# Delta rule and attention encoder on one core: the order of the matmuls taken from an estimate of all engines, outputs of four chunks at once, squares summed in batches, decay tables made inside each batch

## The chip, the core and the metric

The kernel runs on one core of one Trainium2 chip. The core has five engines that run at the same time and meet at semaphores: TensorE (PE in the profile; its weight loads have a row of their own, PEld), VectorE (DVE), ScalarE (ACT), GpSimd (POOL) and SyncE (SP), which here only issues DMAs. ACT issues DMAs too. Each engine works through its own instructions in a fixed order. The metric is the device time of one execution in microseconds, the median of several runs.

## The reference, cut to what matters

One step of a two-layer streaming encoder on 1024 prompt frames and 64 sample frames, all float32. Layer 0 has gated convolutions and chunk-band attention of 8 heads. Layer 1 is a gated DeltaNet with 8 heads of 128 x 128; its frames are cut into chunks of 64, and each chunk needs the state S that the chunk before it left:

```python
def gdn_chunk(S, q, k, v, g, beta):
    gc = jnp.cumsum(g, axis=1)
    ...
    decay = jnp.exp(jnp.where(incl, gct[..., :, None] - gct[..., None, :], -jnp.inf))
    kk = jnp.einsum('blhd,bmhd->bhlm', k, k)
    a = jnp.where(strict, bt[..., :, None] * kk * decay, 0.0)
    tmat = a + jnp.eye(L, dtype=a.dtype)
    rhs = jnp.swapaxes(jnp.concatenate([v * beta[..., None], k * (beta * jnp.exp(gc))[..., None]], axis=-1), 1, 2)
    sol = lax.linalg.triangular_solve(tmat, rhs, left_side=True, lower=True, unit_diagonal=True)
    u = sol[..., :HD_C] - jnp.einsum('bhlk,bhkv->bhlv', sol[..., HD_C:], S)
    qk = jnp.einsum('blhd,bmhd->bhlm', q, k) * decay
    o = jnp.einsum('blhk,bhkv->blhv', q * jnp.exp(gc)[..., None], S) + jnp.einsum('bhlm,bhmv->blhv', qk, u)
    k_dec = k * jnp.exp(g_last[:, None, :] - gc)[..., None]
    S_new = jnp.exp(g_last)[..., None, None] * S + jnp.einsum('blhk,bhlv->bhkv', k_dec, u)
    return S_new, o
```

q and k are L2-normalised before this, and o goes through an RMS norm per head, is multiplied by silu(z) and projected back to 1024 channels. Each layer adds an RMS-normalised result to x.

## The kernel before

**The stages.** Frames lie along the free axis in three groups of 384, 384 and 320 columns. A projection of one weight tile (128 output channels) and one group is 24 matmuls: 8 slices of the contraction, three matmuls each, since weights and activations are split into a high and a low part (`whi`, `wlo`, `hhi`, `hlo`). The core runs, one after the other: the input norm and the projections of layer 0 with the attention of head pairs between them (`even`), the output projection of layer 0 with its norms (`out`), layer 1 (`odd`: convolution tiles of q, k, v per pair of heads with the delta rule between them, then 8 `gate` tiles of z), and the output projection of layer 1. The weights stream in through `stage` on SP's queue; ACT makes the high part and DVE the low part.

**The order of PE.** Only PE's order is written out by hand; the other engines' instructions are ordered by a scheduler of the language. PE's order comes from `Order`: every piece of work is a generator with a rank, and `Order.run` always advances the piece of the lowest rank that is due. A generator yields a number of nanoseconds (not before so long from now), or the name of another piece that must be done first. The piece `main` (rank 5) holds all projections. `project` yields 0 after two of the three matmuls of each slice, and there another piece may step in. The clock of `Order` is a sum of costs that `mm` and `tr` add for PE alone (n / 2.4 + 3 ns for an F32R matmul of n columns); what DVE, ACT, POOL and the DMAs do stands only in the constants that the generators yield, written by hand.

**The delta rule.** A pair of heads p has 17 chunks (16 of the prompt, one of the sample) in batches of 6, 6 and 5, so there are 12 batches. Pieces per batch: `prepare` (rank 2) transposes k and q of each chunk (`tr`), takes the squares' sums with one ACT instruction per chunk (L884), and makes the matrices `An` and `KQD` from `Dst` and `DT`, the decay tables. `substitute` (1.6) inverts 16 x 16 blocks on POOL in 28 small operations (L930, L931), with a DMA to DRAM and back ahead of it (`Sd`, `AL`) and one more pair behind it (`Sd`, `Xf`). `join` (1.5) puts the blocks together in four visits of PE, of which the first needs `XT`, the transpose of what came back. `solve` (1.3) applies the inverse. `scan` (1) goes through the chunks: `ks` = k and q times S, then `us` on DVE (L1079), `su` = the state's update, then the new S on DVE (two operations, L1093). The outputs of a chunk, `up`, are computed ahead of the next chunk's `ks`, added to `qs` on DVE (L1048) and squared on ACT (L1052). `finish` (3) scales four chunks by their norm (one DVE operation per chunk, L1114), transposes them and stores them.

**The decay tables** of all 12 batches are made by the piece `decays` (rank 3) straight after `gates`: per batch one DVE product, one matmul against C_BD, one DVE difference, then two POOL operations (L841), two ACT exponentials and two DMAs to DRAM (`Dd`) on ACT's queue. `prepare` loads its two tables back on SP's queue. The scratch `dbuf` takes one of the two buffers that v uses (`vt`), so `main` waits for `decays` before it makes v of the second pair.

**Waits of main.** q and k of a pair (`kq`) have two buffers, so `main` starts pair p only when `scan` of pair p-2 has ended, and the gates only when the third pair's has.

## Time and profile before

| what | value |
|---|---|
| median of 3 runs | 1499.7 us (1496.54 to 1502.31) |
| the profiled execution, its own time | 1498.51 us |
| its span in the profile | 1496.7 us |
| granted TensorE clock, mean | 0.973 |

The span is the time from the first to the last instruction; 1.8 us of the profiled execution's time lie outside it. Busy time of an engine excludes its DMA issues and its waits. Matmuls overlap, so two matmuls that each take 0.34 us can start 0.17 us apart: where PE is concerned, the distance between starts and the idle time say more than the durations. The granted clock is the share of its full clock that TensorE had; in this profile it is either whole or half.

### The profile page before, as it was taken

Reading aid. Unit: us, or ns where it says so; the run is one execution under the profiler, and the core shown is the slowest. Engines: PE = TensorE matmul, PEld = TensorE weight load, DVE = VectorE, ACT = ScalarE, POOL = GpSimd, SP = SyncE. Lnnn points to the kernel's source line nnn. Section 1 sums busy time; section 2 is a strip of 40 time slices with the busy share of each in tenths; the row PEclk is TensorE's granted clock in tenths of the full one; section 3 lists DMA queues with packets and bytes.
Section 4 is the critical chain, followed back from the end, with each engine's and each line's share of the span. In section 5 each row is a group of like instructions: output and inputs, shape, how many; then the busy total and the mean of one; then the engine's idle time right before and its main releaser. Section 6 shows DMA issues by size and latency. Waiting matters only on the chain. (4 is left out here: it accounts for less than half of the span.)

```text
span 1496.7 us, 28755 instructions
## 1 busy us (share of the span) xinstructions
PE 1376.2 (92%) x10578; PEld 1237.4 (83%) x10578; DVE 858.7 (57%) x2400; ACT 745.6 (50%) x1948; POOL 402.1 (27%) x909
## 2 busy tenths in 40 slices
PE   4899999999999999898876999999989989999995
PEld 3888998999999899887765877778877778888985
DVE  6647237326525755776675667664756665443654
ACT  6544144235325456776655566556555644323642
POOL 4100000000000014432447254452645261410322
PEclk9999999999999999998987999999999999999998
DMA  5231210220211174541332112211211132337454
GB/s 201 83 114 44 77 58 26 87 65 29 74 61 58 44 233 149 180 146 36 94 87 63 31 51 57 42 41 47 67 35 41 37 96 60 99 108 238 154 190 156
DMA packets 114381, 133.15 MB, mean 89 GB/s; under 512 B 35568, under 2 KB 81336, under 8 KB 114240
## 3 DMA queue, kind: packets, MB, share of 16 engines
q1 hardware_dynamic: 82128, 101.86, 22.9%
q10 hardware_dynamic: 32112, 29.45, 6.1%
q8 instruction: 83, 1.36, 0.4%
q14 instruction: 58, 0.48, 0.1%
HBM read 99.91 MB, written 34.51 MB: 90 GB/s over the span
## 5 line engine op out<-in xcount | busy, mean ns | idle before, releaser
L119 PE MATMUL pjt<-hhi,wlo 128*128 128x384 f32 (+1 forms) x1768 | 621.4, 351 | 1.8 <-DVE wlo L162 1.8
L119 PE MATMUL pjt<-hhi,whi 128*128 128x384 f32 (+1 forms) x1768 | 587.5, 332 | 19.7 <-ACT ko L464 4.2
L119 PE MATMUL pjt<-hlo,whi 128*128 128x384 f32 (+1 forms) x1768 | 586.8, 332 | 7.3 <-DVE hlo L215 6.6
L119 PEld LDWEIGHTS pjt<-hhi,whi 128*128 128x128 f32 x1768 | 340.4, 193 | 29.1 <-ACT hhi L214 6.6
L119 PEld LDWEIGHTS pjt<-hhi,wlo 128*128 128x128 f32 x1768 | 340.3, 192 | 26.0 <-issue 12.2
L119 PEld LDWEIGHTS pjt<-hlo,whi 128*128 128x128 f32 x1768 | 339.0, 192 | 10.5 <-DVE hlo L215 8.8
L162 DVE TENSOR_TENSOR wlo<-wf,whi 128x512 fp32r<-128x512 f32 x222 | 155.6, 727 | 138.3 <-ACT whi L161 137.0
L161 ACT CAST whi<-wf 128x512 fp32r<-128x512 f32 x222 | 129.9, 619 | 154.7 <-PE pjt L119 110.9
L544 ACT ACTIVATE pr<-pr,mx 128x640 f32<-128x640 f32 (+5 forms) x72 | 50.9, 706 | 92.7 <-DVE mx L543 92.2
L722 POOL TENSOR_TENSOR kq<-kq,tap 128x384 f32<-128x384 f32 (+1 forms) x64 | 49.7, 784 | 140.5 <-DVE kq L719 99.5
L505 POOL MEMSET bias<- 64x64 f32 x8 | 1.5, 187 | 315.4 <-DMA bias<-Gd 245.0
L345 POOL TENSOR_TENSOR sqa<-sqa,sq 128x384 f32<-128x384 f32 (+1 forms) x36 | 39.7, 1103 | 150.1 <-ACT sq L343 150.0
L541 DVE CUSTOM_DVE_ANT_0 pr<-sc,bias 128x640 f32<-128x640 f32 (+5 forms) x72 | 48.0, 666 | 26.3 <-PE sc L119 22.8
L1093 DVE SCALAR_TENSOR_TENSOR S<-S,egl,su 128x128 f32<-128x128 f32 x128 | 41.1, 343 | 34.9 <-PE su L119 34.3
L930 POOL TENSOR_TENSOR px<-AL 48x14 f32<-48x14 f32 (+6 forms) x168 | 48.6, 289 | 40.0 <-DMA AL<-Sd 31.6
L931 POOL TENSOR_TENSOR AL<-AL,px 48x14 f32<-48x14 f32 (+6 forms) x168 | 52.4, 312 | 8.7
L719 DVE SCALAR_TENSOR_TENSOR kq<-raw,par,kq 128x384 f32<-128x384 f32 (+1 forms) x96 | 48.7, 526 | 9.9 <-ACT raw L715 9.7
L610 POOL TENSOR_TENSOR cvo<-cvo,th 128x384 f32<-128x384 f32 (+1 forms) x12 | 12.0, 999 | 142.6 <-DVE mx L543 113.3
L884 ACT ACTIVATE junk<-tr 128x128 f32<-128x128 f32 x136 | 38.0, 279 | 19.8 <-PE tr L124 16.5
L124 PE MATMUL pt<-cst,pr 128*128 128x128 f32 (+1 forms) x280 | 43.2, 270 | 4.4 <-DVE pr L546 2.9
L119 PE MATMUL pjt<-mhi,whi 128*128 128x384 f32 x128 | 43.5, 340 | 3.1 <-ACT mhi L161 3.1
L119 PE MATMUL pjt<-mlo,whi 128*128 128x384 f32 x128 | 43.7, 342 | 0.3 <-DVE mlo L162 0.3
(240 smaller groups left out, 2344.5 us busy)
## 6 DMA issues: line engine op xcount, KB each, us to landing
wf<-in_w_in SPq DMA_DIRECT2D x128, 256.0 KB, 3.2
wf<-in_w_out SPq DMA_DIRECT2D x96, 256.0 KB, 3.4
mf<-mixd SPq DMA_DIRECT2D x32, 192.0 KB, 3.5
x<-in_x SPq DMA_DIRECT2D x8, 384.0 KB, 5.3
xg<-in_x SPq DMA_DIRECT2D x2, 1536.0 KB
xd<-xg SPq DMA_DIRECT2D x2, 1536.0 KB, 6.9
Dd<-dbuf ACTq DMA_DIRECT2D x16, 192.0 KB, 2.2
od<-o ACTq DMA_DIRECT2D x12, 256.0 KB, 2.5
```

The costliest lines, as they stand in the source:

```text
L119: return self.pe.matmul(out, lhsT=lhsT, rhs=rhs, start=start, stop=stop, **k)
L124: return self.pe.transpose(out, in_, self.ident[0:k, 0:k])
L161: self.act.copy(out=hi, in_=x)
L162: (eng or self.dve).tensor_tensor(lo, x, hi.bitcast(F32), ALU.subtract)
L345: pool.tensor_tensor(acc, acc, sq, ALU.add)
L541: dve.tensor_tensor_reduce(out=cut(pr[0:nq, :nk]), in0=sc[0:nq, :nk // nw, :nw], in1=cut(b["bias"][a][0:nq, j0:j0 + nk]), scale=1.0, scala ...
L544: act.activation(pr[0:nq, :nk], pr[0:nq, :nk], AF.Exp, bias=mx[0:nq, 1:2], scale=1.0, accum_out=mx[0:nq, 2:3])
L719: dve.scalar_tensor_tensor(o, ch(raw[:, i0 + j:i0 + j + m]), cw[j], o, ALU.mult, ALU.add)
L722: pool.tensor_tensor(o, o, ch(t), ALU.add)
L930: pool.tensor_tensor(t, AL[:, j + 1:16, j:j + 1].broadcast_to([lanes, m, w]), x.broadcast_to([lanes, m, w]), ALU.mult)
L931: pool.tensor_tensor(o, o, t, ALU.add)
L1093: dve.scalar_tensor_tensor(Sn[:, q, :], S[:, q, :], egl[:, q, p, c:c + 1], su[q], ALU.mult, ALU.add)
```

## The change

1. **A clock for all engines.** The class `Clock` keeps, for every tensor, when each region was last written and read, and for DVE, ACT, POOL and the DMAs a list of busy spans. `Meter` wraps each engine, so that every operation passes through `Clock.other`, which takes its duration from a fixed part and a part per element; `mm` and `tr` pass through `Clock.tensor`, which waits for its operands and adds 200 ns where the shape of the used array changes. `Pool` wraps the tile pools and tells when a buffer comes free (`turn`).
2. **What generators yield.** No constants any more, but the list of tiles and buffers that the next step needs. `Order.due` takes the latest of their estimated times and adds a margin: 300 ns up to rank 1.1, 1500 ns up to rank 3.5, none for main. `project` now yields twice per slice of the contraction.
3. **Outputs** of up to four chunks become a piece of their own (`out`, rank 2.5): the matmuls of the four, one DVE addition, one ACT square, one DVE sum.
4. **Squares** in `prepare` are taken by one ACT operation per four chunks and summed by one DVE reduction.
5. **Decay tables** are made at the head of `prepare`, in the buffers of `An` and `KQD`, with no DMA; the piece `decays`, its scratch and main's wait for it are gone.
6. `An` is scaled by `sA` on POOL, and `finish` scales its four chunks with one POOL operation. Two DVE operations of `scan` are marked as of high priority for the scheduler. `prepare` of a batch also waits for the outputs of the batch three before it.

The core of the diff:

```diff
+class Clock:
+    FIXED = {"DVE": 170, "ACT": 210, "POOL": 260}
+    EACH = {"DVE": 1.04, "ACT": 0.84, "POOL": 1.9}
+    NEAR, PSUM, DMA, BYTES = 60, 190, 2000, 190.0
...
+    def place(self, eng, t, took):
+        b = self.spans.setdefault(eng, [])
...
+        k = len(b)
+        while k and b[k - 1][1] > t:
+            k -= 1
+        while k < len(b) and b[k][0] < t + took:
+            t = max(t, b[k][1])
+            k += 1
+        b.insert(k, (t, t + took))
+        return t + took
+
+    def tensor(self, out, ins, cost, shape, more):
+        t = max([self.now] + [self.ready(x) for x in ins] + ([] if more else [self.over(out, "PE", False)]))
+        if shape != self.shape:
+            t += 200
+            self.shape = shape
+        self.now = t + cost
...
+    def other(self, eng, op, outs, ins):
+        t = max([self.ready(x, eng) for x in ins] + [self.over(x, eng, False) for x in outs])
+        if "dma" in op:
+            at = self.place("DMA", t, outs[0].nbytes() / self.BYTES if callable(outs[0].nbytes) else outs[0].nbytes / self.BYTES) + self.DMA
+            eng = "DMA"
+        else:
+            n = max(x.free_size() for x in outs[:1] + ins)
+            took = self.FIXED[eng] + self.EACH[eng] * n + (200 if len(outs) > 1 else 0)
+            at = self.place(eng, t, took)
...
 class Order:
+    LATE = ((1.1, 300), (3.5, 1500), (9, 0))
...
+    def due(self, t):
+        at = 0.0
+        late = next(x for r, x in self.LATE if t[0] <= r)
+        for x in t[4]:
+            at = max(at, (x() if callable(x) else self.clock.ready(x)) + late)
+        return at
...
     def project(self, w, ops, n, m=P, ks=range(KT)):
+        yield [self.bank_turn, w[0][:, ks[0], :], ops[0][ks[0]]]
...
             hi, lo = ops[0][k], ops[1][k]
+            yield [w[0][:, k, :], w[1][:, k, :], hi, lo]
             o = ps[0:m, :n]
             self.mm(o, w[0][:, k, :], hi, k == ks[0], False)
             self.mm(o, w[0][:, k, :], lo, False, False)
-            yield 0
+            yield ()
             self.mm(o, w[1][:, k, :], hi, False, k == ks[-1])
...
         def prepare(p, b):
-            nc.sync.dma_start(Dst, Dd[2 * p][:, c0:c0 + nb, :])
-            nc.sync.dma_start(DT, Dd[2 * p + 1][:, c0:c0 + nb, :])
+            An, KQD = bt("An", 64, 2), bt("KQD", 64, 3)
+            Dst, DT = An, KQD
...
+            dve.tensor_tensor(Dst, gcb, cst[:, C_ID64:C_ID64 + 64].unsqueeze(1).broadcast_to(sh), ALU.mult)
+            yield [Dst, turn("tr")]
+            ps = pst("tr")[:, :64 * nb]
+            self.mm(ps, cst[:, C_BD:C_BD + P], Dst.rearrange("p c j -> p (c j)"))
+            dve.tensor_tensor(DT, ps.rearrange("p (c j) -> p c j", j=64), gcb, ALU.subtract)
+            for x, cm, op in ((Dst, C_M1, ALU.subtract), (DT, C_M2, ALU.add)):
+                pool.tensor_tensor(x, cst[:, cm:cm + 64].unsqueeze(1).broadcast_to(sh), DT, op)
+                act.activation(x, x, AF.Exp)
+            yield [kq[:, :, c0:c0 + nb]]
...
-                    for i in range(m):
-                        act.activation(junk, ps[:, i, :], AF.Square, accum_out=ss[:, a, i0 + i:i0 + i + 1])
+                    sq = self.kp.tile([P, 4, P], F32, name="sqk", tag="vr")[:, :m, :]
+                    act.activation(sq, ps[:, :m, :], AF.Square)
...
+                    dve.tensor_reduce(ss[:, a, i0:i0 + m], sq, mybir.AxisListType.X, ALU.add)
...
-                for i in range(m):
-                    dve.scalar_tensor_tensor(An[:, i0 + i, :], ps[:, i, 0:64], sA[:, i0 + i:i0 + i + 1], Dst[:, i0 + i, :], ALU.mult, ALU.mult)
+                ai = An[:, i0:i0 + m, :]
+                dve.tensor_tensor(ai, ps[:, :m, 0:64], Dst[:, i0:i0 + m, :], ALU.mult)
                 dve.tensor_tensor(KQD[:, i0:i0 + m, :], ps[:, :m, 64:128], DT[:, i0:i0 + m, :], ALU.mult)
-                yield 510
+                pool.tensor_tensor(ai, ai, sA[:, i0:i0 + m].unsqueeze(2).broadcast_to([P, m, 64]), ALU.mult)
...
         def scan(p, b):
+                    yield [S, kq[:, :, c], vt[:, c, :], turn("ks")]
                     ks = pst("ks")
...
+                    with tc.high_priority():
+                        dve.tensor_tensor(u, ks[:, 0:P], vt[:, c, :], ALU.add)
+                    act.activation(o4[:, a, :], ks[:, P:2 * P], AF.Copy, scale=egc[:, p, c:c + 1])
-                    yield 850
...
+                yield [u, kd[:, i, :], turn("su")]
...
+        def outputs(p, b, i0, m, o4, u4, us, fresh, f):
+            KQD = R[p, b]["KQD"]
+            yield [*us, o4[:, fresh:m], turn("up")]
+            o = pst("up").rearrange("p (c j) -> p c j", j=P)
+            for i in range(m):
+                for q in range(2):
+                    h = slice(64 * q, 64 * q + 64)
+                    self.mm(o[h, i, :], KQD[h, i0 + i, :], us[i][h], share=1.6, tile_position=(64 * q, 64 * q))
...
+            dve.tensor_tensor(o4[:, fresh:m, :], o[:, fresh:m, :], o4[:, fresh:m, :], ALU.add)
+            act.activation(u4[:, :m, :], o4[:, :m, :], AF.Square)
+            so = self.kp.tile([P, 3, 4], F32, name="so", tag="so", bufs=3)
+            dve.tensor_reduce(so[:, 0, :m], u4[:, :m, :], mybir.AxisListType.X, ALU.add)
+            order.add("fin" + f, 3, finish(p, b, i0, m, o4, so), [])
...
         def finish(p, b, i0, m, o4, so):
-            for i in range(m):
-                dve.tensor_scalar(o4[:, i, :], o4[:, i, :], fa[:, i:i + 1], None, ALU.mult)
-            yield 9000
+            pool.tensor_tensor(o4[:, :m, :], o4[:, :m, :], fa.unsqueeze(2).broadcast_to([P, m, P]), ALU.mult)
+            yield [o4, turn("tr")]
```

Attention and the norms of `out` get lists in place of constants in the same way (before, for instance, the second head's scores waited 1010 ns and the transposes of a unit's probabilities 3000 ns after them).

More of the change, by code (lines that the diff above doesn't have):

```diff
@@ new lines, with __init__, __getattr__, call @@
+class Meter:
+    def __init__(self, clock, eng, real):
+        self._clock, self._eng, self._real = clock, eng, real
+    def __getattr__(self, name):
+        real = getattr(self._real, name)
+        if not callable(real):
+            return real
+        def call(*a, **k):
+            r = real(*a, **k)
+            aps = {i: x for i, x in enumerate(a) if hasattr(x, "tensor")} | {i: x for i, x in k.items() if hasattr(x, "tensor")}
+            outs = [aps.pop(i) for i in ("out", "accum_out") if i in aps]
+            if aps and (not outs or "out" not in k):
+                first = next(iter(aps))
+                outs.insert(0, aps.pop(first))
+            if outs:
+                self._clock.other(self._eng, name, outs, list(aps.values()))
+            return r
+        return call
@@ L90, in run @@
             self.live.sort(key=lambda t: t[:2])
-            free = [t for t in self.live if not (t[5] - self.done)]
-            ready = [t for t in free if t[4] <= self.now]
+            free = [(t, self.due(t)) for t in self.live if not (t[5] - self.done)]
+            ready = [t for t, at in free if at <= self.clock.now]
             if not ready:
-                self.now = min(t[4] for t in free)
+                self.clock.now = min(at for _, at in free)
                 continue
@@ L122, in tr @@
         k = in_.partition_size()
-        self.order.now += 108 if k > 64 else 56
+        self.clock.tensor(out, [in_], 109 if k > 64 else 62, (-(-k // 32), 4), False)
         return self.pe.transpose(out, in_, self.ident[0:k, 0:k])
@@ L218, in open @@
         es = ExitStack()
[L219 removed]
+        p = Pool(self.clock, es.enter_context(self.tc.tile_pool(name=name, bufs=1, **(dict(side=side, reuse_waits="tile") if not k else k))))
         self.opened[name] = es
```

274 lines of the change are left out of this document (153 added, 121 removed).

## The prediction

> **What bounds the kernel now.** I read the page's head first, then busy time by stage, then PE's waits inside the two stages of layer 1 that the change rewrites, then single stretches of the timeline. The stage rows give length and PE, PEld, DVE, ACT and POOL busy (with counts), the granted clock, DMA share and GB/s.
>
> ```profile
> span 1496.7 us, 28755 instructions
> ```
> ```profile
> 100.00:600.00 500.00, 492.63 (x3371) 467.60 (x3369) 257.24 (x687) 211.05 (x486) 31.68 (x38) 1.00 0.24 76
> 600.00:712.00 112.00, 101.70 (x625) 90.52 (x624) 83.37 (x158) 77.43 (x153) 38.05 (x32) 0.96 0.37 121
> 712.00:825.00 113.00, 85.32 (x600) 75.79 (x600) 75.25 (x182) 63.88 (x173) 61.04 (x106) 0.88 0.32 81
> 825.00:1350.00 525.00, 499.07 (x4918) 418.57 (x4918) 310.58 (x1151) 274.14 (x893) 217.97 (x679) 0.98 0.22 59
> ```
>
> PE is the engine to save: in the scan stage (825 to 1350) it is busy 95%, DVE only 59%. The work that PE does hardly changes in amount, so the change can win only PE's idle time, and the half clock that follows it. Attention (100 to 600) leaves 7.4 us idle in 500: little to win there. The ramp into the delta rule (712 to 825) leaves 113 - 85.32 = 27.7 us, the scan stage 525 - 499.07 = 25.9 us; together 53.6.
>
> The half clock: these rows are the stretches at half clock between 702 and 822 us (the first of five, and their sum), then the sum of the three after 1060.
>
> ```profile
> 702.00:712.60 10.60, 8.48 (x86) 8.11 (x86) 5.11 (x16) 4.36 (x9) 1.98 (x2) 0.52 0.01 2
> ...
> sum 38.10, PE 27.91 PEld 24.58 DVE 20.94 ACT 16.29 POOL 18.45; mean PE 5.58 PEld 4.92 DVE 4.19 ACT 3.26 POOL 3.69
> ```
> ```profile
> sum 17.20, PE 12.81 PEld 12.31 DVE 10.53 ACT 8.43 POOL 13.60; mean PE 4.27 PEld 4.10 DVE 3.51 ACT 2.81 POOL 4.53
> ```
>
> Work at half clock takes twice as long, so half of its busy time is lost: (27.91 - 8.48) / 2 = 9.7 us in the ramp (its first stretch is before the delta rule and stays), 12.81 / 2 = 6.4 us later; together 16.1. So 53.6 + 16.1 = **69.7 us is the most** that these two stages can return without PE doing less.
>
> What PE waited for, longest in total, in the ramp and then in the scan stage (us, times, longest):
>
> ```profile
> PE tr L119 <- DVE XT L960: 9.3, 1, 9.3
> PE tr L124 <- DVE dbuf L838: 5.4, 2, 3.7
> PE tr L119 <- DVE kd L887: 4.9, 1, 4.9
> ```
> ```profile
> PE tr L124 <- DVE o L1114: 7.2, 3, 5.3
> ...
> PE tr L119 <- DVE XT L960: 2.9, 2, 1.9
> ...
> PE su L119 <- DVE us L1079: 1.3, 2, 0.9
> ```
>
> These are visits whose written delay was shorter than reality: PE is in order, so a transpose of `finish` sent 5.3 us too early (`o`) stops projections that were ready. The scan itself is almost never late (`us` twice, 1.3 us): its constants are generous.
>
> **The change, part by part.**
>
> *Order from an estimate.* Waits of the kind "my constant did not know that DVE or POOL was busy" should go. What the estimate can't see is an engine's queue held by a DMA: it puts each operation into the engine's next free time. The trace shows such a case, on POOL:
>
> ```profile
> 782.47 0.21 POOL L930 TENSOR_TENSOR px<-AL 48x14 f32<-48x14 f32 x1 [5.14 <-DMA AL<-Sd]
> ```
>
> POOL stood 5.1 us for `AL`; the convolution's additions queued behind it, then DVE, and PE's 4.9 us wait for `kd` followed. The `XT` waits hang on the same chain. The estimate takes 2000 ns plus bytes / 190, for these 48 KB 2.26 us; measured landings (`AL`, then `Xf`):
>
> ```profile
> DMA to landing us min/median/max: 1.6/2.4/5.6
> ```
> ```profile
> DMA to landing us min/median/max: 2.2/3.2/4.8
> ```
>
> The median errs by 0.1 and 0.9 us, inside the margin of 1.5; the slow hops don't. So I keep the waits of this family, 9.3 + 4.9 + 2.9 = 17.1 of 53.6, **32%**, and let the rest go: -36.5 us. The half clock goes in the same share: -10.9. Bounds: nothing kept (-69.7), two thirds kept (-23). What is late next is `AL` and `Xf`.
>
> *Visits.* What it costs PE to leave a projection:
>
> ```profile
> 909.78 0.31 PE L119 MATMUL pjt<-hhi,whi 128*128 128x320 f32 x1
> 909.93 0.31 PE L119 MATMUL pjt<-hlo,whi 128*128 128x320 f32 x1
> 910.17 0.44 PE L119 MATMUL up<-us,KQD 64*64 64x128 f32 x4
> 910.53 0.66 PE L119 MATMUL ks<-S,kq 128*64 128x128 f32 x8
> 911.12 0.42 PE L119 MATMUL pjt<-hhi,wlo 128*128 128x320 f32 x1
> 911.37 0.31 PE L119 MATMUL pjt<-hhi,whi 128*128 128x320 f32 x1
> ```
>
> Projections start 0.15 us apart; the last before the visit has 0.24, the first after it 0.25: about 0.2 us a visit. `up` takes 0.36 for four records, `ks` 0.59 for eight, so four more records cost 0.23. Outputs now: 68 x 0.36 = 24.5 us. After: 68 x 0.23 + 24 visits x (0.13 + 0.2) = 23.5. **Batching the outputs is worth 1 us of PE.** Against it, steps that shared a visit because their constants fell together now come due one by one, and a unit of attention gets a separate visit for its fifth key tile. I take +6 us, some 30 visits; the trace can't show how many, so the bounds are -4 (20 merge) and +15 (75 more). Net +5.
>
> *Decay tables.* Per batch the same two DVE operations, matmul, two POOL operations and two exponentials; 24 stores on ACT's queue and 24 loads on SP's go.
>
> ```profile
> L841 POOL TENSOR_TENSOR dbuf<-cst,dbuf x24: 857/1110/1315, 723.8 to 805.2; 128x384 f32<-128x384 f32 x16, 128x320 f32<-128x320 f32 x8
> ```
>
> All 24 stood in the ramp; now about six do, so some 18 x 1.11 = 20 of POOL's 61 busy us leave it. That is part of why the ramp's waits go and isn't counted again. Main's wait for `decays` is free: with the ramp's waits gone main has eight tiles ahead of it, by the code, and the scan of the first pair runs meanwhile; if that scan ends later than main's tiles, PE idles as long as it is late, inside the range up to some 10 us. The new wait of `prepare` for outputs three batches back costs nothing: a whole batch's scan lies between.
>
> *Squares and scalings.*
>
> ```profile
> L884 ACT ACTIVATE junk<-tr 128x128 f32<-128x128 f32 x136 | 38.0, 279 | 19.8 <-PE tr L124 16.5 <-DVE raw L710 0.6 <-ACT junk L884 0.4
> ```
> ```profile
> L887 DVE TENSOR_TENSOR kd<-tr,dec 128x512 f32<-128x512 f32 x12 | 8.2, 686 | 3.9 <-ACT kt L886 3.8
> ```
> ```profile
> L722 POOL TENSOR_TENSOR kq<-kq,tap 128x384 f32<-128x384 f32 x32 | 32.5, 1015 | 95.9 <-DVE kq L719 61.3 <-DVE so L1108 14.8 <-DVE so L1109 9.0
> L896 POOL TENSOR_TENSOR kt<-kt,kap 128x768 f32<-128x768 f32 x8 | 12.2, 1523 | 5.9 <-DVE sA L894 3.4 <-DVE kap L895 2.4
> ```
>
> ACT loses 136 squares of 279 ns with their read-outs and gets 48 wider ones: relief. DVE gets 48 reductions and 24 for the outputs. No row shows a reduction; the nearest DVE operation of 512 elements takes 686 ns, half of them are that wide, the rest half or less: about 37 us (bounds 20 and 50), which the operations given to POOL and the merged additions about repay. POOL gets 48 scalings, between the rows for 384 and 768 elements 1.2 us at 512: about 37 us. In the scan stage DVE is busy 310.58 and POOL 217.97 of 525, so all lies beside PE: 0, and the rival below if that cover fails.
>
> *Norms of `out`.* Three waits of 600 to 712 hang on the squares' sums and should go: -2 of these 2.8 us.
>
> ```profile
> PE pjt L119 <- POOL sqa L345: 1.0, 1, 1.0
> PE pjt L119 <- ACT sq L343: 0.9, 1, 0.9
> PE pjt L119 <- POOL sqb L314: 0.9, 1, 0.9
> ```
>
> **Sum:** 1496.7 - 36.5 - 10.9 + 5 - 2 = 1452.3 us of span; with the 1.8 us outside it (1498.5 for the profiled execution) **1454 us**. That execution lies 1.2 us below the median of 1499.7, which I neglect.
>
> **The rivals.**
>
> *A. More goes.* The late landings were a result of the crowded ramp and leave with it; 55 to 70 us gone: 1426 to 1440. For it: the typical landings fit the estimate. Against: by the code these DMAs share SP's queue with the weights all along.
>
> *B. POOL holds up DVE.* One DVE operation of 0.31 us median took 1.05 while a POOL addition ran:
>
> ```profile
> 767.87 1.07 POOL L722 TENSOR_TENSOR vt<-vt,tap 128x384 f32<-128x384 f32 x1 [1.02 <-ACT junk L884]
> ```
> ```profile
> 768.00 1.05 DVE L912 SCALAR_TENSOR_TENSOR Af<-An,cst,Af 128x96 f32<-128x96 f32 x1
> ```
> ```profile
> L912 DVE SCALAR_TENSOR_TENSOR Af<-An,cst,Af x36: 284/310/1070, 768.0 to 1268.1; 128x96 f32<-128x96 f32 x24, 128x80 f32<-128x80 f32 x12
> ```
>
> The estimate gives each operation a fixed time. If each of the 48 new POOL scalings (0.77 us on average) holds a DVE operation ahead of a scan step for its whole length, less the 0.3 us margin, that is 48 x 0.47 = 23 us: 1477. Against it: the median of the 36 says that most go free.
> The Trainium skill ("SBUF — State Buffer", Who interferes with whom) says that DVE and GpSimd share one pair of SBUF ports, held by one for a whole instruction, and that a DVE operation with two SBUF inputs contends with GpSimd's reads; it speaks against giving POOL work. The row agrees: 1.05 against 0.31 us.
>
> *C. It doesn't do what it says.* PE's order is planned, but the other engines' order still comes from a scheduler that the estimate doesn't know; the waits move and stay as large: 1498, between 1490 and 1507. Against: the estimate's parts fit the rows closely.
>
> *D. Slower: the scan's margin is too thin.* Before, the scan's steps left 850 and 1110 ns on a clock that ran slow (it gave 136 ns to a matmul that takes 0.15 us). Now a scan step is sent 300 ns after its estimate. DVE is in order and often within a weight split:
>
> ```profile
> L162 DVE TENSOR_TENSOR wlo<-wf,whi 128x512 fp32r<-128x512 f32 x222 | 155.6, 727 | 138.3 <-ACT whi L161 137.0 <-PE tr L124 0.5
> L1079 DVE TENSOR_TENSOR us<-ks,vt 128x128 f32<-128x128 f32 x64 | 18.4, 288 | 20.3 <-PE ks L119 13.8 <-ACT raw L715 6.2
> L1093 DVE SCALAR_TENSOR_TENSOR S<-S,egl,su 128x128 f32<-128x128 f32 x128 | 41.1, 343 | 34.9 <-PE su L119 34.3 <-issue 0.2
> ```
>
> There are 136 scan visits (`ks` and `su` of 68 chunks), and while PE waits nothing else runs. It decides against the change from a mean lateness of 46 / 136 = 0.34 us beyond the margin. A whole split each time, 0.7 us: 95 us, net +49: 1547. For it: DVE is busy 59% of that stage. Against: the estimate allows 190 + 303 + 60 + 300 = 853 ns after `ks` where `us` takes 288, and 1156 after `su` where two S take 686, so half a microsecond is left; and the operations got priority.
>
> **How the numbers follow.** Forecast (1440 to 1475) 0.58; A 0.12; B (1475 to 1492) 0.10; C 0.08; D 0.12. Predicted is the forecast's 1454. Faster by over 0.5% (under 1492; 7.5 us is about what a measurement of this kernel can tell from no change): 0.58 + 0.12 + 0.10 = 0.80; within 0.5% 0.08; slower 0.12. The range: below, A's bound, 1425 (0.03 left out beyond it); above, into C, 1500, with D and the rest of C left out, 0.15.
>
> **What would show each step.** Idle PE between 712 and 1350 falls from 53.6 to some 17 us, with `XT` or what hangs on `AL` first among the waits, and `o` and `dbuf` gone; half clock after 712 is under 15 us; `up` comes in records of 16 and PE's busy time in the scan stage hardly falls per chunk; ACT falls by some 65 us and POOL rises by some 40. It would be wrong if `su` or `ks` head the waits (D), if L1079 or L1093 start late behind POOL (B), if idle time stays near 50 us under other names (C), or if main stands still for a scan to end.

## The result and the profile after

The changed kernel takes 1549.0 us (1541.9 to 1551.3), beside 1501.0 us of the kernel before in the same session: 1.0306 times the time, with a 95% interval of 1.0251 to 1.0361. It is slower by some 48 us, and the forecast of 1454 was wrong in its sign.

The page's head, first; then, from both kernels, busy time by stage, cut at the same events in each: the first matmul of `gates`, the first `su`, the last `su`, the first matmul of the last output projection. Columns as before: window, its length, busy us of PE, PEld, DVE, ACT and POOL with counts, granted clock, DMA share, GB/s.

```profile
span 1549.5 us, 28339 instructions
...
PE 1397.2 (90%) x10578; PEld 1267.6 (82%) x10578; DVE 877.2 (57%) x2320; ACT 732.1 (47%) x1630; POOL 431.4 (28%) x957
```
Before:
```profile
705.00:834.00 129.00, 101.32 (x745) 91.72 (x745) 83.14 (x203) 72.54 (x193) 64.62 (x112) 0.86 0.30 75
834.00:1336.00 502.00, 476.07 (x4766) 396.38 (x4764) 299.97 (x1116) 264.06 (x867) 210.25 (x650) 0.98 0.22 58
1336.00:1369.00 33.00, 33.00 (x205) 32.23 (x204) 11.94 (x33) 9.36 (x22) 5.14 (x24) 1.00 0.50 163
```
After:
```profile
719.00:837.00 118.00, 105.40 (x811) 98.91 (x811) 74.13 (x198) 62.66 (x147) 50.45 (x101) 0.93 0.19 40
837.00:1372.00 535.00, 473.32 (x4615) 398.22 (x4613) 321.75 (x1033) 257.73 (x589) 255.45 (x705) 0.91 0.18 44
1372.00:1417.00 45.00, 45.00 (x278) 44.40 (x278) 14.85 (x38) 11.98 (x26) 6.24 (x26) 1.00 0.46 143
```

The 53 us of span stand in five places. Up to `gates` 14 are lost (705 to 719). The ramp is 11 us shorter (129 to 118), as hoped: its idle PE fell from 27.7 to 12.6 us. The scan stage is 33 longer (502 to 535), and its idle PE is 535 - 473.3 = 61.7 us, before 25.9. Behind it stand 12 more (33 to 45), projections that PE did not get to earlier. The last projection takes the other 5. In the scan stage PE did 151 matmuls less, and the clock fell from 0.98 to 0.91.

Over the whole span, counted in the two traces: PE's idle time went from 120.4 to 152.2 us. Half of the time that PE was busy at half clock is lost; this went from 28.0 to 64.3 us. The rest of PE's busy time, its work at full clock, went from 1348.2 to 1333.0 us. So PE had 15 us less to do and lost 68 us more, over half of that to the clock.

What PE waited for in the scan stage after, longest in total (us, times, longest):

```profile
PE tr L285 <- POOL o L186: 24.5, 8, 4.9
PE su L280 <- DVE u L186: 9.8, 10, 3.0
PE tr L280 <- DVE XT L186: 6.2, 3, 3.7
PE ks L280 <- DMA S<-in_s: 6.0, 4, 2.0
...
PE ks L280 <- DVE S L186: 2.4, 4, 0.9
```

In these waits an instruction had been put into PE's fixed order too early. All waits of this view add up to 60.8 of the 61.7 idle us. They don't show whether PE had anything else to do: there are stretches in which `main` has no projection to offer. PE's timeline at the longest (start, us, tiles; rows left out between):

```profile
912.77 0.31 PE L280 MATMUL pjt<-hhi,wlo 128*128 128x320 f32 x1
913.20 0.53 PE L280 MATMUL tr<-M,X 32*32 32x16 f32 x40
918.09 0.69 PE L285 MATMUL tr<-cst,o 128*128 128x128 f32 x2 [4.36 <-POOL o L186]
...
922.17 2.05 PE L280 MATMUL tr<-BD,kt 128*128 128x128 f32 x8 [0.25 <-DVE BD L186]
...
927.24 0.66 PE L280 MATMUL ks<-S,kq 128*64 128x128 f32 x8
...
946.77 1.06 PE L280 MATMUL tr<-vr,BD 128*128 128x128 f32 x8
947.75 0.44 PE L280 MATMUL up<-u,KQD 64*64 64x128 f32 x4
948.12 0.44 PE L280 MATMUL pjt<-hhi,whi 128*128 128x384 f32 x1
```

For 35 us there is no projection (`pjt`): by the code, `main` has finished the second pair's tiles and waits for the first pair's scan to end before it starts the third's. A second such stand, 32 us, comes before the `gate` tiles. PE has only the delta rule's small steps then, each behind another engine, and much of it runs at half clock: `tr<-BD,kt` takes 2.05 us where its eight matmuls take 1.13 elsewhere. The rows of the two stands:

```profile
913.10:948.10 35.00, 26.56 (x363) 20.55 (x363) 19.09 (x55) 15.71 (x39) 8.00 (x22) 0.71 0.15 35
1227.10:1259.60 32.50, 25.49 (x278) 18.71 (x278) 14.81 (x43) 13.63 (x33) 8.97 (x20) 0.63 0.19 56
```

PE is idle 8.4 and 7.0 us in them, 15.5 of the stage's 61.7. The other 46.2 us lie where projections were at hand; before, the whole stage had 25.9. So the stands are about a quarter of the idle time, and neither kind of loss is the whole.

The scan itself was late. `ks` is its first visit for a chunk; these are its visits on both sides of the border between the first pair's second and third batch, before and after:

```profile
882.93 0.66 PE L119 MATMUL ks<-S,kq 128*64 128x128 f32 x8
905.70 0.61 PE L119 MATMUL ks<-S,kq 128*64 128x128 f32 x8
```
```profile
897.28 0.92 PE L280 MATMUL ks<-S,kq 128*64 128x128 f32 x8
927.24 0.66 PE L280 MATMUL ks<-S,kq 128*64 128x128 f32 x8
```

The scan stands 22.8 us before and 30.0 after, until the third batch is ready. Over the 64 visits of each trace, the 11 distances across a border between batches or pairs add up to 243.9 us before and 260.3 after, and the 52 distances within a batch to 253.7 and 271.5. So batches come later, and within a batch the chunks follow each other more slowly as well, by about the same total. The length of `prepare`, from a batch's first transpose of k to its last `Af`, is read from such rows (batch 2, before, then after):

```profile
834.73 0.66 PE L124 MATMUL tr<-cst,kq 128*128 128x128 f32 x4
...
858.07 0.30 DVE L912 SCALAR_TENSOR_TENSOR Af<-An,cst,Af 128x80 f32<-128x80 f32 x1
```
```profile
842.11 0.66 PE L285 MATMUL tr<-cst,kq 128*128 128x128 f32 x4
...
877.41 0.28 DVE L186 SCALAR_TENSOR_TENSOR Af<-An,cst,Af 128x80 f32<-128x80 f32 x1
```

From 23 to 35 us in this batch; on average over the 12, up to the store of `Af`, from 24.7 to 30.9 us. The decay tables are not in this stretch: they come ahead of the first transpose.

### The profile page after: what moved, and what is told of

It is laid out like the page before. It is cut to its first block, busy times and chain, and to the rows that moved or that the text cites. A ratio compares the mean times of both kernels' runs of the same rounds, so it can differ in the third digit from the quotient of the medians.

```text
span 1549.5 us, 28339 instructions
## 1 busy us (share of the span) xinstructions
PE 1397.2 (90%) x10578; PEld 1267.6 (82%) x10578; DVE 877.2 (57%) x2320; ACT 732.1 (47%) x1630; POOL 431.4 (28%) x957
## 5 line engine op out<-in xcount | busy, mean ns | idle before, releaser
L280 PE MATMUL pjt<-hhi,whi 128*128 128x384 f32 (+1 forms) x1768 | 604.3, 342 | 31.4 <-ACT raw L186 11.7
L280 PE MATMUL pjt<-hhi,wlo 128*128 128x384 f32 (+1 forms) x1768 | 607.9, 344 | 3.1 <-DVE wlo L186 2.9
L280 PEld LDWEIGHTS pjt<-hlo,whi 128*128 128x128 f32 x1768 | 343.1, 194 | 11.1 <-DVE hlo L186 8.8
L186 DVE TENSOR_TENSOR wlo<-wf,whi 128x512 fp32r<-128x512 f32 x222 | 159.7, 744 | 153.6 <-ACT whi L186 152.9
L186 POOL TENSOR_TENSOR sqa<-sqa,sq 128x384 f32<-128x384 f32 (+1 forms) x43 | 44.7, 1040 | 201.7 <-ACT sq L186 184.5
L186 POOL TENSOR_TENSOR so<-so 128x4 f32<-128x4 f32 (+2 forms) x216 | 50.3, 235 | 127.0 <-DVE so L186 116.3
L186 POOL TENSOR_TENSOR px<-AL 48x14 f32<-48x14 f32 (+6 forms) x168 | 53.1, 316 | 41.9 <-DMA AL<-Sd 26.0
L280 PE MATMUL ks<-S,kq 128*64 128x128 f32 x512 | 48.9, 307 | 8.7 <-DMA S<-in_s 6.0
L186 ACT ACTIVATE o<-ks,egc 128x128 f32<-128x128 f32 x64 | 23.5, 367 | 57.9 <-DVE u L186 55.6
L280 PEld LDWEIGHTS ks<-S,kq 128*64 128x64 f32 x512 | 31.7, 148 | 23.1 <-issue 15.4
L186 ACT ACT_TABLE_LOAD x38 | 48.8, 1283 | 3.8 <-DMA Gd<-Ld 2.4
```

The source lines that it names most:

```text
L186: r = real(*a, **k)
L280: return self.pe.matmul(out, lhsT=lhsT, rhs=rhs, start=start, stop=stop, **k)
```

## The experiments

Two theories stood at the start. **PE's waits**: the estimate sends steps too early (to `finish` behind POOL, to the scan behind DVE), and what PE stands idle is lost. **Late batches**: the chain of a batch got longer, `main` runs out of projections and PE has nothing to do. Each run has beside it the kernel before on the same chip; "stage" is the stretch from the first to the last `su`, by the rows of busy time by stage.

| run | us | ratio to before | stage us, idle PE, clock |
|---|---|---|---|
| before | 1501 | 1 | 502, 25.9, 0.98 |
| after | 1549 | 1.0306 [1.0251, 1.0361] | 535, 61.7, 0.91 |
| b_out4 | 1503 | 1.0030 [1.0014, 1.0046] | 502, 32.2, 0.98 |
| b_pool | 1517 | 1.0124 [1.0100, 1.0149] | 519, 37.7, 0.97 |
| b_decays | 1527 | 1.0197 [1.0172, 1.0223] | 550, 46.8, 0.95 |
| order_only | 1540 | 1.0253 [1.0230, 1.0276] | 514, 55.8, 0.92 |
| b_late6 | 1538 | 1.0247 [1.0210, 1.0284] | 538, 45.7, 0.95 |
| b_exps | 1505 | 1.0000 [0.9979, 1.0022] | 506, 28.2, 0.98 |
| b_tables | 1500 | 1.0018 [1.0000, 1.0036] | 503, 26.7, 0.98 |
| o_dve | 1540 | 1.0243 [1.0209, 1.0277] | 516, 60.6, 0.93 |
| late300 | 1550 | 1.0314 [1.0279, 1.0350] | 554, 67.3, 0.91 |
| decays_ahead | 1553 | 1.0341 [1.0313, 1.0369] | 519, 70.2, 0.91 |
| fin9000 | 1552 | 1.0337 [1.0290, 1.0384] | 536, 69.2, 0.91 |
| fin9000_rest300 | 1554 | 1.0344 [1.0292, 1.0396] | 567, 75.2, 0.90 |
| fin9000_scan800 | 1520 | 1.0117 [1.0079, 1.0155] | 531, 50.6, 0.94 |
| fin9000_scan1500 | 1586 | 1.0585 [1.0553, 1.0616] | 604, 99.5, 0.90 |
| scan800 | 1530 | 1.0203 [1.0180, 1.0226] | 527, 50.6, 0.94 |
| odd_fixed | 1619 | 1.0772 [1.0729, 1.0814] | 617, 111.1, 0.89 |
| est_dve | 1554 | 1.0372 [1.0345, 1.0399] | 557, 69.6, 0.90 |
| est_best | 1593 | 1.0637 [1.0605, 1.0669] | 606, 92.4, 0.88 |

### One part of the change alone, on the kernel before

**b_out4.** Outputs of four chunks in one visit, with the priority of the scan's operations, and with delays as before.

```diff
-                if last:
-                    outputs(*last)
+                if a == 3 or i == nb - 1:
+                    order.add("out" + f, 2.5, outputs(p, b, i - a, a + 1, o4, u4, us, ...), [])
```


> The kernel before with one part of the change: outputs of four chunks per visit, with their squares summed in a batch, and priority for the scan's operations; order and delays as before. What the prediction costed at 1 us less of PE: 1495 to 1506. If the new body is harmful by itself: over 1512.

1503 us, slower by 0.3%. PE is busy 469.8 us in the stage instead of 476.1, and idle 32.2 instead of 25.9: what the batching saves of PE, its waits take back.

**b_pool.** The two scalings on POOL.

```diff
-            for i in range(m):
-                dve.tensor_scalar(o4[:, i, :], o4[:, i, :], fa[:, i:i + 1], None, ALU.mult)
+            pool.tensor_tensor(o4[:, :m, :], o4[:, :m, :], fa.unsqueeze(2).broadcast_to([P, m, P]), ALU.mult)
...
+                pool.tensor_tensor(ai, ai, sA[:, i0:i0 + m].unsqueeze(2).broadcast_to([P, m, 64]), ALU.mult)
```


> The kernel before with one part of the change: the scalings of the outputs (per four chunks) and of An done by POOL. The prediction had them beside PE: within 8 us of 1502. If POOL in order is the mechanism (the scalings queue behind a substitution, and what comes behind them waits): `tr` for `o` or for `XT` takes 30 us or more, and the time is 1515 to 1560.

1517 us, slower by 1.24%, inside the range expected for POOL's order as the mechanism, though neither wait reached the 30 us named there. The two largest among PE's waits, over the whole span:

```profile
PE tr L119 <- DVE XT L961: 25.3, 4, 16.1
PE tr L124 <- POOL o L1114: 12.9, 3, 7.9
```

`XT` was 12.2 us before and `o` (on DVE) 7.2. Both hang on POOL, one on the substitution, one on the new scaling: POOL goes through its queue in order, and its load, 234 of 519 us, says nothing of how long the queue is when a batch needs it.

**b_decays.** The decay tables inside `prepare`, with the delays of the old piece.

```diff
-            nc.sync.dma_start(Dst, Dd[2 * p][:, c0:c0 + nb, :])
-            nc.sync.dma_start(DT, Dd[2 * p + 1][:, c0:c0 + nb, :])
+            dve.tensor_tensor(Dst, gcb, cst[:, C_ID64:C_ID64 + 64].unsqueeze(1).broadcast_to(sh), ALU.mult)
+            yield 900
+            ps = pst("tr")[:, :64 * nb]
...
+            yield 2500
```


> The kernel before with one part of the change: the decay tables computed in each batch's prepare. The ramp up to the first `su` gets 5 to 15 us shorter, since 18 of POOL's 24 operations leave it. If the longer chain in each batch and the table loads cost nothing: 1485 to 1500. If they cost what the ramp gives or more: 1500 to 1530, with `XT` or `KQD` first among the waits.

1527 us. Its ramp and its scan stage:

```profile
703.00:810.00 107.00, 92.94 (x732) 86.89 (x732) 63.12 (x185) 58.57 (x170) 43.15 (x91) 0.89 0.17 35
810.00:1360.00 550.00, 503.19 (x4805) 413.88 (x4804) 312.48 (x1140) 303.47 (x913) 229.59 (x670) 0.95 0.18 48
```

The ramp is 22 us shorter and the scan stage 48 longer. What the ramp returns, every batch pays later. The waits are headed by `o` (16.6 us), not by `XT` or `KQD` as expected. `main` never runs out for more than 8 us in this scan stage: its 46.8 idle us, 21 more than before, are mostly PE's waits while projections were at hand, and the clock fell from 0.98 to 0.95. Why, b_late6 and b_exps ask.

**order_only.** The order by the estimate, around the bodies of before (also the decays ahead). The edit is shown against the changed kernel.

```diff
-                    sq = self.kp.tile([P, 4, P], F32, name="sqk", tag="vr")[:, :m, :]
-                    act.activation(sq, ps[:, :m, :], AF.Square)
+                    for i in range(m):
+                        act.activation(junk, ps[:, i, :], AF.Square, accum_out=ss[:, a, i0 + i:i0 + i + 1])
...
+                if last:
+                    outputs(*last)
...
-            pool.tensor_tensor(o4[:, :m, :], o4[:, :m, :], fa.unsqueeze(2).broadcast_to([P, m, P]), ALU.mult)
+            for i in range(m):
+                dve.tensor_scalar(o4[:, i, :], o4[:, i, :], fa[:, i:i + 1], None, ALU.mult)
...
+                        order.add("decays", 3, decays(), ["gates"])
```

> The order from the estimate, with the margins of the changed kernel, around the bodies of before: outputs per chunk inside the scan, squares with their sums on ACT, decays ahead, scalings on DVE and not on POOL. If the bodies are to blame (POOL's scaling, decays, batches of outputs): 1445 to 1475, what the prediction gave for the order alone. If the order itself is (1500 ns at every step of a batch, 300 ns at the scan's): over 1520, with main standing still for a scan to end.

1540 us: the order alone loses 2.5%. But its longest stand is not of the kind expected. `main` stands from 853 to 933 us, and comes back right behind the last matmul of `decays` (932.5). The last of the 24 POOL operations of `decays` starts at 936.8:

```profile
L186 POOL TENSOR_TENSOR dbuf<-cst,dbuf x24: 852/993/1453, 739.1 to 936.8; 128x384 f32<-128x384 f32 x16, 128x320 f32<-128x320 f32 x8
```

In the kernel before the last starts at 805.2. By the code, `decays` has rank 3, and each of its visits waits until one of the two `tr` banks has been free for 1500 ns; every other piece of the batch wants the same banks at a better rank. So this run holds a loss of its own that the changed kernel hasn't, and its 38 us are no clean price of the order.

### Is it lateness, or work?

**b_late6.** The kernel before; each `prepare` starts 6 us later on the order's clock, and nothing else is added.

```diff
-            yield 4000 if b == 0 else 0
+            yield 10000 if b == 0 else 6000
```


> The kernel before, with one number changed: prepare of each batch starts 6000 ns later on the order's clock; no engine does more. If the delta rule goes by when its batches are ready: the scan's stands between batches (258.6 us in all now) grow by 20 to 60 us, main stands for a scan, and the time is 1515 to 1550. If there is slack in the batches, and PE's waits for late operands are what costs: within 6 us of 1500.

1538 us, 2.5% slower, 37 us: no instruction was added, and PE, DVE and POOL have the kernel before's work (counts in the stage of 4761, 1116 and 652 beside 4766, 1116 and 650).

```profile
832.00:1370.00 538.00, 492.26 (x4761) 406.97 (x4759) 297.90 (x1116) 262.81 (x864) 210.54 (x652) 0.95 0.21 55
```

Idle PE went from 25.9 to 45.7 us and the clock from 0.98 to 0.95: both follow from late batches here. The distances between `ks` across a border grew from 243.9 to 273.5 us, within a batch from 253.7 to 260.3. So this run decides one thing: the batches have no slack that 6 us wouldn't use up. It doesn't decide between the theories, since `main` stands only once for more than 8 us:

```profile
926.60:947.40 20.80, 11.85 (x169) 8.04 (x168) 12.28 (x52) 10.12 (x45) 6.51 (x21) 0.61 0.26 49
```
```profile
PE tr L124 <- DVE o L1114: 16.5, 7, 4.5
```

That stand holds 8.9 of the 45.7 idle us. The rest are waits of PE, `o` first, which took 7.2 before: late batches cost through such waits as well.

**b_exps**, and **b_tables** before it. Two exponentials of one column in each batch, to bring in the activation table loads of the decays alone.

```diff
+            for q in range(2):
+                e = self.kp.tile([P, 1], F32, name="e1", tag="e1", bufs=2)
+                act.activation(e, rr[:, q, 0:1], AF.Exp, scale=-1.0)
```


> The kernel before, with two exponentials of one column in each batch's prepare, whose results nothing uses: they add what the decays inside the batch add in activation table loads (from 20 to about 40, 1.28 us each) and nothing else. If the table loads are the cost of the decays: 1515 to 1530. If the longer chain is: within 6 us of 1501.

> The kernel before, with two exponentials of one column in each batch's prepare, tied to the batch by reading its norms; nothing uses their results. Table loads go from 20 to 32 or more. If the loads (1.28 us each on ACT) are the cost of the decays inside the batch: 1512 to 1530. If the longer chain is: within 6 us of 1500.

In b_tables the exponentials read `gc`, which is there from the start; the loads stayed at 20, so they must have been put beside other exponentials, and the run says nothing. In b_exps they read the batch's norms. ACT's groups of table loads, in b_exps and then the same lines of before:

```profile
L729 ACT ACT_TABLE_LOAD x12 | 15.4, 1283 | 0.9 <-ACT dbuf L842 0.8
L895 ACT ACT_TABLE_LOAD x10 | 12.8, 1283 | 0.2
```
```profile
L729 ACT ACT_TABLE_LOAD x3 | 3.8, 1283 | 0.8 <-ACT dbuf L842 0.8
```

That and one more make 40 loads instead of 20, as many as in b_decays. ACT is busy 30 us more (775.6 beside 745.6), and the time is the same, 1.0000 [0.9979, 1.0022]. The Trainium skill ("ScalarE: Activation LUTs", What ACT_TABLE_LOAD costs) gives 1283 ns a load, as the rows do, and 2.66 us for a switch with its drain; by that figure 20 switches would be 53 us, an estimate, if ACT were on the path. The time shows that it isn't: 20 more loads on ACT cost nothing when nothing waits for the exponentials. In b_decays the batch does wait for them, and no run took that alone. What is left for the decays' 30 us, by elimination and so not shown, is the longer way of each batch (two delays of 0.9 and 2.5 us and the work between them, on POOL too) and the waits of PE that follow.

### The margins

Here only `LATE` and, for the scan, its rank change.

```diff
-    LATE = ((1.1, 300), (3.5, 1500), (9, 0))
+    LATE = ((3.5, 300), (9, 0))                                    late300
+    LATE = ((1, 300), (1.1, 800), (3.5, 1500), (9, 0))             scan800, scan at rank 1.05
+    LATE = ((1.1, 300), (2.9, 1500), (3.5, 9000), (9, 0))          fin9000
+    LATE = ((2.9, 300), (3.5, 9000), (9, 0))                       fin9000_rest300
+    LATE = ((1, 300), (1.1, 800), (2.9, 300), (3.5, 9000), (9, 0)) fin9000_scan800; 1500 for 800: fin9000_scan1500
```


> The changed kernel with 300 ns instead of 1500 ns of margin for the batch's steps (solve, join, substitute, prepare, outputs, finish). Late batches by margin: prepare has eight or so visits, each 1.2 us earlier, so a batch is ready some 10 us sooner, the two stands of main (35.6 and 34.1 us) shrink to 20 to 25 each, and the time falls to between 1520 and 1535. Late scaling and thin margin: the transposes of `finish` come sooner after POOL was asked and wait longer, `tr` for `o` goes from 24.5 to over 30 us, and the time is 1549 or up to 15 us more.

> The changed kernel, but `finish` sends its transposes 9000 ns after the estimate has the scaled outputs ready instead of 1500; POOL still scales. Too early a finish: the 24.5 us of waits of `tr` for `o` go, and with each of the eight waits one stretch of about 3.4 us at half clock (1.7 us lost): 1549 falls by 24 to 38 us, to between 1511 and 1525. POOL's load itself: the waits move to what else hangs on POOL (AL, kq, vt) and the time stays above 1540. If only main's two stands for a scan decide, the waits were inside them and the time falls by less than 10 us.

late300: 1550, as without it. Its waits and those of fin9000:

```profile
PE tr L285 <- POOL o L186: 39.6, 11, 7.8
```
```profile
PE tr L280 <- DVE XT L186: 32.3, 7, 13.4
PE su L280 <- DVE u L186: 12.9, 11, 3.0
```

Less margin brings `prepare` down only from 30.9 to 28.8 us and PE into waits for POOL. Main's two stands mostly go: in the scan stage, stretches of over 8 us without a projection add up to 30 us instead of 68, with the same time. A late `finish` takes the `o` waits away (3.4 us are left); PE waits for `XT` instead and `main` stands longer (112 us in all), at 1552. So neither the stands nor one of the waits is what the time hangs on: taking one away moves the loss to the other.

> As fin9000, and with 300 ns instead of 1500 for all the batch's other steps. If the batches' margins and the early finish both cost: main's stands go as they did with 300 ns alone, and no `o` waits come in their place: 1475 to 1500. If the 1500 ns cost nothing (as 300 ns alone, which gave 1550, may say): the same as fin9000 within 8 us.

> The changed kernel with one number changed: the scan's own steps come 800 ns after the estimate instead of 300, all other margins as they were. If the scan's thin margin is the mechanism (PE stands for `u` or `S`, and half clock follows): waits of `su` and `ks` on DVE fall from 12 to under 5 us, half clock between the first and the last `su` by some 10 us, and the time by 15 to 30 us, to between 1519 and 1534. If its gain with the other margins was chance or needs the late finish: 1541 or more.

> As fin9000_rest300, and the scan's own steps 800 ns instead of 300 after the estimate. Thin margin of the scan (the prediction's case of slower): the 12 us of waits of `su` and `ks` go and what follows them at half clock, 10 to 18 us less than fin9000_rest300. If the margin is right: a chunk's two visits come 0.5 us later each, 68 chunks are 68 us longer in a chain that main's projections must fill, main stands longer for a scan, and it is 5 to 20 us more than fin9000_rest300.

> fin9000_scan800 with 1500 instead of 800 ns behind the estimate for the scan's steps. If steps sent too early are what costs: another 5 to 20 us less, 1500 to 1515. If 800 covers them: the scan's chain gets 136 x 0.7 us longer, main runs out of projections and stands longer, 1525 to 1550.

fin9000_rest300: 1554, as fin9000. scan800: 1530, within what the thin margin was expected to cost, but not for its reason. `su` waits for `u` as long as it did:

```profile
PE su L280 <- DVE u L186: 10.0, 13, 2.0
```

Idle PE in the stage falls by 11 us: outside main's two stands from 46 to 27 us, while the stands remain (46 and 25 us). The clock goes from 0.91 to 0.94. `prepare` is as long as without the 800 ns (30.7 us on average), so 19 of the 48 us came back without the batches getting shorter. With the late `finish` and 300 ns elsewhere the same 800 brings 34 us. And 1500 instead of 800 costs 66, more than was expected either way:

```profile
817.00:1421.00 604.00, 504.49 (x4831) 431.95 (x4832) 327.48 (x1060) 266.52 (x614) 246.35 (x712) 0.90 0.17 45
```

99.5 us idle. The chain of 68 chunks is then the later one: the distances between `ks` within a batch add up to 519 us, those across borders to 77.5 (351 and 175 with 800). So there is an optimum that depends on the other margins; where it lies, and why 800 helps, stays open.

### Parts of the change taken back

**o_dve**: the outputs' scaling on DVE again. **decays_ahead**: the piece `decays` again. **odd_fixed**: the new bodies with the old written delays in the delta rule.

```diff
o_dve
-            pool.tensor_tensor(o4[:, :m, :], o4[:, :m, :], fa.unsqueeze(2).broadcast_to([P, m, P]), ALU.mult)
+            for i in range(m):
+                dve.tensor_scalar(o4[:, i, :], o4[:, i, :], fa[:, i:i + 1], None, ALU.mult)
decays_ahead
+                        order.add("decays", 3, decays(), ["gates"])
...
+            nc.sync.dma_start(Dst, Dd[2 * p][:, c0:c0 + nb, :])
+            nc.sync.dma_start(DT, Dd[2 * p + 1][:, c0:c0 + nb, :])
odd_fixed
-                    yield [S, kq[:, :, c], vt[:, c, :], turn("ks")]
...
-                yield [u, kd[:, i, :], turn("su")]
+                if S is not None:
+                    yield 850
...
-            yield [o4, turn("tr")]
+            yield 9000
```

> The changed kernel, with the scaling of the outputs (o4) by DVE per chunk again instead of by POOL per four chunks. Three theories for the 49 us that the change lost. Late scaling: PE's transposes of `finish` wait for POOL, which is in order and busy with a substitution's 28 operations; then the 24.5 us of waits of `tr` for `o` go, with the half clock behind them, and the time falls from 1549 to between 1510 and 1525. Late batches: main runs out of projections because the batches come late for other reasons; then PE waits for something else or stands longer at the ends of main's tiles, and the time stays above 1538. Thin margin of the scan: DVE gets 68 more operations of about 0.2 us ahead of the scan's steps; the waits of `su` and `ks` grow from 12 to some 20 us and the time is 1549 or more.

> The changed kernel with the decay tables computed ahead for all pairs, stored to DRAM and loaded per batch, as before the change. If the decays inside the batch are to blame (activation table loads went from 20 to 38, 1.28 us each, and every batch has a longer chain ahead of its transposes): prepare of the third batch of a pair falls from some 40 to some 28 us, the two stands of main shrink from 35 to 15 us, table loads fall to about 20, and the time is 1510 to 1525. If they are not: within 8 us of 1549, the ramp up to 10 us longer again.

> The changed kernel's bodies, but in the delta rule (gates, prepare, substitute, join, solve, scan, outputs, finish) each step comes a written delay after the last, with the numbers of before (9000 ns for finish, 850 and 1110 for the scan, 2160 per group of prepare); attention and norms keep the estimate. If the estimate in the delta rule is the cause: idle PE plus half clock between the first and the last `su` fall from 101 us to between 35 and 50, and the time to between 1480 and 1500. If the new bodies are the cause (POOL's scalings, decays inside the batch): above 1525.

o_dve: 1540, 9 us less with intervals that overlap, not the 24 and more that its waits had promised; `tr` now waits 14.1 us for `o` from DVE. decays_ahead: 1553, no gain, since the piece starves as in order_only (the last of its POOL operations starts at 905 us). odd_fixed: 1619, on the side expected if the new bodies are the cause (above 1525), but not a clean test of it. The old delays don't fit the new bodies: `XT` alone takes 70.9 us of waits there and `o` 37.1. The estimate is better than those constants for these bodies; it is the old bodies under the old constants that beat both.

**est_dve** and **est_best** start from fin9000_scan800, put both scalings on DVE, and then make the decays ahead (rank 2.9).

```diff
est_dve
-                pool.tensor_tensor(ai, ai, sA[:, i0:i0 + m].unsqueeze(2).broadcast_to([P, m, 64]), ALU.mult)
+                    dve.scalar_tensor_tensor(An[:, i0 + i, :], ps[:, i, 0:64], sA[:, i0 + i:i0 + i + 1], Dst[:, i0 + i, :], ALU.mult, ALU.mult)
est_best
+                        order.add("decays", 2.9, decays(), ["gates"])
```

> fin9000_scan800 (1520 us), with the scalings of the outputs and of An on DVE instead of POOL. By what POOL's scalings cost alone (19 us): 1500 to 1510, with the waits of `tr` for `XT` down from 18 to under 10 us. If they cost nothing under this order: 1515 or more.

> est_dve, with the decay tables computed ahead again. By what the decays inside the batch cost alone (30 us): 1475 to 1495, faster than both kernels; table loads fall from 36 to 20 to 28. If the order by the estimate keeps a loss of its own: 1500 to 1520, with main still standing for a scan over 25 us.

Both went the other way, 1554 and 1593. To take POOL's scalings back cost 34 us here, where they cost 19 by themselves in b_pool; why stays open. In est_best `main` stands 45, 61, 17 and 36 us, and the scan stage shows it:

```profile
822.00:1428.00 606.00, 513.65 (x4846) 441.88 (x4842) 342.47 (x1157) 253.42 (x605) 218.24 (x665) 0.88 0.21 55
```

The parts cost 4, 19, 30 and 38 us one by one, 91 in sum, and 48 together; taken back one by one under the estimate's order they return 9, nothing, or cost more. They don't add. The 38 hold the starving of `decays`, which the changed kernel hasn't; beyond that, each edit shifts the whole order behind it, and that they draw on the same slack is argued, not shown. No run beat the kernel before.

## Why the prediction was wrong, point by point

**The step that failed** is the two large terms of the sum, -36.5 us of waits that "go" and -10.9 of half clock. Measured over the span, idle PE rose by 32 us and the loss by half clock by 36; in order_only, with the bodies of before, by 25 and 31. The estimate removed some waits and made others (`o`, `u`, `S`), and waits of 2 us lower the clock too (last section).

**What bounds the kernel** is where this came from. "PE is the engine to save", and 69.7 us of idle PE and half clock "is the most" to return: that counted PE's share and took its 95% for the only limit, so idle time could only be won. The scan stage also goes by a pair's chain, from `prepare` through POOL's substitution, `join` and `solve` to the scan. b_late6 shows it for the kernel before: 6 us later per batch, 37 us of time, no work added. For the changed kernel it is argued from `prepare`, 6.2 us longer on average; how much of the 48 us is the chain, and how much the order's early steps, no run separates.

**What lay "beside PE" at 0** failed with it. POOL's scalings cost 32.5 us of POOL's time (19.2 and 13.3 by the groups of POOL; the prediction had 37) and 19 us of the kernel's in b_pool, where PE waits for what stands in POOL's queue. The decays at 0, "part of why the ramp's waits go": the ramp did shrink, by 22 us in b_decays, and the scan stage grew by 48. The table loads that they bring, 18 more in the changed kernel, were overlooked; b_exps shows that such loads cost nothing by themselves. ACT's busy time fell by 13 us and not by some 65: that figure left out the wider squares (22.6 us), and these loads (23 us) come on top.

**"Main's wait for `decays` is free"** and, if the scan ends later, idle "up to some 10 us": the wait for the scan came, two stands of 35 and 32 us, and the text named a `main` that "stands still for a scan to end" as what would make it wrong. The mechanism was in it; the size was wrong, for want of the batch's length as a term of the sum: 15.5 us idle and, at clocks of 0.71 and 0.63, another 18 lost.

**The waits.** `dbuf` went. `XT` fell from 12.2 to 6.8 us, no longer first. `o` did not go but rose from 7.2 to 24.5, now behind POOL. Idle PE from the first matmul of `gates` to the last `su` rose from 53.6 to 74.3 us instead of falling to 17; the half clock rose with it. The waits for `out`'s sums did not go: `sq` alone takes 2.4 us there after, 0.9 before.

**Visits**, net +5: the sign was wrong. PE's work at full clock fell by 15 us instead. Counted in the scan stage, PE leaves a projection for other work 165 times among 1346 of main's matmuls, before 204 times among 1519. `up` comes in records of 16, as foreseen; batched alone (b_out4) the outputs save 7 us of PE's work, not 1, and it bought nothing.

**The rivals.** B (POOL, 1477) had the right engine and the wrong place. In b_pool DVE's operations take what they took before (the new S 342 ns, before 343; `Af` 350, before 371), so nothing of a held DVE shows in these rows; `XT` and `o` wait for what POOL makes. B's 1477 was faster than before; b_pool was slower. D said 1547 and the time is 1549, but its price was made of PE's waits behind DVE in 136 visits; these are 12.2 us (9.8 for `u`, 2.4 for `S`), not 95. The margin is worth 19 us by scan800, where the wait for `u` stayed at 10 us, so not by D's way. The number is right by chance.

**Left open.** The 14 us before `gates` stand in every run with the estimate's order (`gates` starts at 714 to 721 us; with written delays at 703 to 707), also in odd_fixed, where only attention and norms keep the estimate. So they come from there: over a quarter of the loss, in stages where the prediction saw "little to win" and counted 2 us won. Attention ends with `main` out of projections (518.6 to 532.2 us), but no run took that part alone. The squares were not run alone. Nor was a third buffer for q and k tried, which by the code would let `main` start a pair earlier.

## What to carry to other kernels

An engine that is busy 95% need not be the only limit if a low-ranked filler makes the 95%: look for the chain beside the filler, and test it by making one link late without adding work. A cost "beside" the busy engine is free only if the chain through that other engine has slack; in the kernel before, 6 us per batch were 37 us of kernel. And prices of parts taken alone need not add: 91 us one by one were 48 together. Idle time on the busiest engine is no upper bound of what an order can lose: count the clock with it.

## What the runs showed of the hardware

A short wait costs more than its length. PE's clock changes in steps of some 3.4 us; these are three neighbouring stretches of the changed kernel (PE's busy time and the granted clock), with the wait that stands in the first:

```profile
1045.40:1048.80 3.40, 1.82 (x17) 1.27 (x14) 2.72 (x9) 1.20 (x3) 2.67 (x7) 1.00 0.00 0
1048.80:1052.20 3.40, 3.40 (x17) 2.62 (x17) 0.73 (x4) 1.21 (x3) 2.00 (x11) 0.50 0.14 51
1052.20:1055.60 3.40, 3.40 (x26) 2.40 (x25) 2.10 (x6) 2.05 (x6) 1.14 (x4) 1.00 0.08 26
```
```profile
1048.73 1.07 PE L285 MATMUL tr<-cst,o 128*128 128x128 f32 x4 [1.58 <-POOL o L186]
```

PE idled 1.58 us in one stretch, was busy 1.82 us of it, and had half its clock for the whole next stretch, though it was busy throughout: 17 matmuls, where the stretch behind it has 26. So the wait of 1.58 us cost another 1.7. It is no single case: cut into such steps, the trace has 24 falls of the clock, and in the step before each PE was busy 2.1 us or less. Some steps of 1.7 to 2.0 us busy were not followed by a fall. The Trainium skill ("TensorE: Matmul & The Clock Gate", What's actually happening) has the clock fall after at least one idle window of about 3.4 us; the length of the steps agrees, but here a stretch that was half busy was enough, and the measurement decides. So an order with many waits of 2 to 3 us can lose more in clock than in idle time, as this one did: 36 us beside 32.
